# Shifting the tiles behind h by 32 bytes in SBUF, so that they start on multiples of 64 bytes

## The chip, the cores and the metric

The kernel runs on one core of one Trainium2 chip. The metric is the device time of one execution in microseconds (us), as the median of several runs. Shares and clocks come from one profiled execution of the same program.

## What is computed

One layer of a hybrid decoder block, for a sequence of 512 rows of width 1024, all in fp32:

```
mod  = silu(c) @ w_ada + b_ada;  shift, scale, gate = split(mod, 3)
h    = rmsnorm(x, norm_g) * (1 + scale) + shift            # 512 x 1024
proj = h @ w_in                                            # 512 x 14344
qm,km,vm,om,zm,im,fm,qa,ka,va,za,gm,ga = split(proj)
qm, km = split(silu(causal_dwconv([qm, km])))
ym = (head_rmsnorm(sigmoid(om) * mlstm(qm,km,vm,im,fm)) * silu(zm)) @ w_proj_m
ya = (head_rmsnorm(diff_attention(qa,ka,va)) * silu(za)) @ w_proj_a
y  = sigmoid(gm) * ym + sigmoid(ga) * ya
out = rmsnorm(x + gate * (y @ w_out), final_g)
```

The matrix memory (mLSTM) has 4 heads, the differential attention 8. By far the most arithmetic is in `h @ w_in`.

## The kernel before

Each fp32 matrix is split into a high and a low part, and a product is made of three matmuls (`mm3`, lines 133 to 142): high by high, high by low, low by high, all into one PSUM tile. In a matmul one operand is loaded into the array as weights (128 columns of it) and the other moves through it (up to 512 columns).

h is kept as two tiles, `h_hi` and `h_lo`, each 8 blocks of 128 x 512, 16384 bytes per partition. The weight matrix is read in 112 pieces of 128 x 1024 (4096 bytes per partition). Each piece passes through a ring of three buffers each (`raw` for the fp32 data as loaded by SyncE's queue, `whi` and `wlo` for its two parts): ScalarE rounds `raw` to `whi` (line 100), VectorE makes `wlo` as the difference (line 118). Then TensorE uses it in one of two ways: `proj_b` (lines 343 to 352) takes ring columns as weights and moves h over them, 24 matmuls of 512 columns for a piece; `mm_v` (lines 354 to 358) takes h as weights and moves ring columns, 48 matmuls of 256 columns for a piece. `attn_proj` and `proj_m` (lines 706 and 744) take ring columns as weights and move `hh` and `hl`, tiles behind h. The attention and mLSTM cores, cut into small steps by generators that `tick()` calls, fill in between. The order of instructions on each engine is the program's own, with some manual dependencies that keep it.

SBUF is laid out in the order in which pools and tiles are made, each tile at a multiple of 32 bytes of a partition. First come the tiles of the pool `const`: the small ones made before h (`sm`, `ident`, `onesf`, `ones_r`, `mod` and others), then an unused tile of 32 bytes (line 338), then `h_hi` at byte 10784 and `h_lo` at 27168, both 32 past a multiple of 64, then a second unused tile of 32 bytes (line 341) and the few small tiles made later (`acol` and others). Behind `const` lies the pool `stg` with the weight ring, from byte 43808, 32 past a multiple of 64, and behind that the pool `sb` with all others. Within both pools every tile that a matmul reads is as large as a multiple of 64 bytes or follows such tiles, so all of them start 32 bytes past a multiple of 64; and the slices that a matmul takes of them begin at multiples of 64 bytes from the start.

Of the kernel before, what the change touches and what calls it, by code (L numbers as in the profile page):

```python
# [9 lines left out]
F32 = mybir.dt.float32  # L10
# [6 lines left out]
P = 128  # L17
# [48 lines left out]
def hybrid_block_kernel(ctx: ExitStack, tc: tile.TileContext, xT, x, c, wada2, wada, win, wif, wpm, wpa, wout,  # L66
# [3 lines left out]
    const = ctx.enter_context(tc.tile_pool(name="const", bufs=1))  # L70
# [196 lines left out]
    for k in range(NK):  # L267
        i, start = (0, k == 0) if k < 5 else (1, k == 5)
# [69 lines left out]
    const.tile([P, 8], F32, name="pad_before")  # L338
    h_hi = const.tile([P, NK, S], F32R, name="h_hi")
    h_lo = const.tile([P, NK, S], F32R, name="h_lo")  # L340
    const.tile([P, 8], F32, name="pad_after")

    def proj_b(col, between=None):
        hi, lo = split_granule(win[GIDX[("B", col)]])
# [242 lines left out]
    for k in range(NK):  # L587
# [23 lines left out]
        else:  # L611
            csl2.append(sb.tile([P, S], F32, tag="hp", bufs=16, name=nm("csl")))
            i = k - NK + 2
# [454 lines left out]
```

## Time and profile before

| | |
|---|---|
| median of 3 runs | 930.69 us (928.89 to 931.09) |
| the profiled execution | 929.48 us, its span 927.3 us |
| TensorE busy | 914.2 us, 99% of the span, 4735 matmuls |
| VectorE busy | 603.1 us, 65% |
| ScalarE busy | 455.0 us, 49% |
| granted TensorE clock, mean | 0.998 of full |

A busy time counts an engine's own instructions and not its waits. Matmuls are pipelined: one is shown with a duration of some 390 ns while the next starts after some 227 ns, so the distance between starts, not the duration, tells how fast they go. Weight loads have an engine label of their own (PEld) and run beside the matmuls. In the names of a group, the part behind the arrow lists what is read (`acc<-h_hi,whi`), in no order that tells which moves; the width does (512 columns: h moves; 256 columns with h: ring columns move).

### The profile page before, as it was taken

How to read it: one execution, taken by the hardware profiler on the slowest of the kernel's cores; microseconds unless marked ns; L12 is line 12 of the kernel's file. 1: busy time of each engine (PE TensorE's matmuls, PEld its weight loads, DVE VectorE, ACT ScalarE, POOL GpSimd, SP SyncE). 2: the span in 40 equal slices, each digit the busy share in tenths (PEclk: the TensorE clock that was granted, in tenths of full speed). 3: DMA queues.
4: the chain of work that ended last, by engine and by line, in shares of the span. 5: the costliest groups of instructions: out<-in, count | busy, mean ns of one | idle time of the engine just before them, and what ended most of it. 6: DMA issues, size and time to landing. Idle time of an engine off the chain costs nothing.

```text
span 927.3 us, 12276 instructions
## 1 busy us (share of the span) xinstructions
PE 914.2 (99%) x4735; PEld 781.6 (84%) x4735; DVE 603.1 (65%) x975; ACT 455.0 (49%) x741; POOL 24.2 (3%) x56
## 2 busy tenths in 40 slices
PE   7999999999999999999999999999999999999997
PEld 3888987988888899888899888898888988888886
DVE  7967888877675465334568444595554866638944
ACT  7556887766667454222356333453233643137422
POOL 0000010000001000000000000000000000000000
PEclk9999999999999999999999999999999999999999
DMA  9873314434332443332222222222131224426421
GB/s 341 335 199 110 132 58 137 143 119 148 125 102 80 138 147 111 139 136 91 91 83 100 91 81 99 70 102 103 69 114 69 92 97 154 142 108 222 142 77 59
DMA packets 40659, 114.95 MB, mean 124 GB/s; under 512 B 8289, under 2 KB 8553, under 8 KB 39578
## 3 DMA queue, kind: packets, MB, share of 16 engines
q1 hardware_dynamic: 40010, 113.11, 35.1%
q10 hardware_dynamic: 592, 1.07, 0.4%
q8 instruction: 37, 0.61, 0.3%
q14 instruction: 20, 0.16, 0.1%
HBM read 106.78 MB, written 10.00 MB: 126 GB/s over the span
## 4 chain that ended last, share of the span: by engine, by line
PE 94%; DVE 2%; DMA 2%; ACT 1%; issue 0%; SPq 0%; ACTq 0%; DVEq 0%
PE acc L135 26%; PE acc L136 26%; PE acc L137 26%; PE core L135 4%; PE core L136 4%; PE core L137 4%; PE core L444 1%; PE core L445 1%; PE core L474 1%; DMA relt<-in_relb_dram 1%; DVE wlo L118 1%; DMA xt<-in_xT_dram 1%; PE core L238 0%; ACT whi L100 0%; DMA raw<-in_win_dram 0%
## 5 line engine op out<-in xcount | busy, mean ns | idle before, releaser
L135 PE MATMUL acc<-h_hi,whi 128*128 128x512 f32 x688 | 269.2, 391 | 0.5 <-DVE qk L412 0.5
L118 DVE TENSOR_TENSOR wlo<-raw,whi 128x1024 fp32r<-128x1024 f32 x129 | 157.7, 1223 | 164.8 <-ACT whi L100 164.8
L100 ACT CAST whi<-raw 128x1024 fp32r<-128x1024 f32 x129 | 135.4, 1049 | 254.0 <-PE acc L136 204.1
L136 PE MATMUL acc<-h_lo,whi 128*128 128x512 f32 x656 | 256.0, 390 | 0.0
L137 PE MATMUL acc<-h_hi,wlo 128*128 128x512 f32 x656 | 255.5, 389 | 0.0
L135 PEld LDWEIGHTS acc<-h_hi,whi 128*128 128x128 f32 x688 | 129.3, 188 | 26.3 <-PE acc L524 0.8
L137 PEld LDWEIGHTS acc<-h_hi,wlo 128*128 128x128 f32 x656 | 123.2, 188 | 26.0
L136 PEld LDWEIGHTS acc<-h_lo,whi 128*128 128x128 f32 x656 | 123.3, 188 | 23.7
L137 PE MATMUL acc<-whi,h_lo 128*128 128x256 f32 x352 | 99.6, 283 | 0.0
L136 PE MATMUL acc<-wlo,h_hi 128*128 128x256 f32 x352 | 99.6, 283 | 0.0
L135 PE MATMUL acc<-whi,h_hi 128*128 128x256 f32 x352 | 99.5, 283 | 0.0
L135 PE MATMUL acc<-hh,whi 128*128 128x512 f32 x192 | 74.8, 389 | 0.0
L136 PE MATMUL acc<-hl,whi 128*128 128x512 f32 x192 | 74.8, 389 | 0.0
L137 PE MATMUL acc<-hh,wlo 128*128 128x512 f32 x192 | 74.7, 389 | 0.0
L136 PEld LDWEIGHTS acc<-wlo,h_hi 128*128 128x128 f32 x352 | 67.4, 192 | 0.7
L135 PEld LDWEIGHTS acc<-whi,h_hi 128*128 128x128 f32 x352 | 67.4, 191 | 0.7
L137 PEld LDWEIGHTS acc<-whi,h_lo 128*128 128x128 f32 x352 | 67.4, 192 | 0.0
L449 ACT ACTIVATE pt<-pt,mn 128x128 f32<-128x128 f32 (+3 forms) x64 | 35.5, 557 | 17.6 <-DVE mn L447 17.4
L137 PEld LDWEIGHTS acc<-hh,wlo 128*128 128x128 f32 x192 | 36.0, 188 | 7.6
L135 PEld LDWEIGHTS acc<-hh,whi 128*128 128x128 f32 x192 | 36.1, 188 | 7.3
L136 PEld LDWEIGHTS acc<-hl,whi 128*128 128x128 f32 x192 | 36.1, 188 | 7.2
L447 DVE CUSTOM_DVE_ANT_0 pt<-core,bt 128x128 f32<-128x128 f32 (+3 forms) x64 | 29.4, 485 | 15.2 <-PE core L445 14.8
(277 smaller groups left out, 1359.9 us busy)
## 6 DMA issues: line engine op xcount, KB each, us to landing
raw<-in_win_dram SPq DMA_DIRECT2D x112, 512.0 KB, 3.3
wa<-in_wada_dram SPq DMA_DIRECT2D x8, 1024.0 KB, 7.0
raw<-in_wpm_dram SPq DMA_DIRECT2D x16, 512.0 KB, 3.3
raw<-in_wada_dram SPq DMA_DIRECT2D x8, 512.0 KB, 3.2
raw<-in_wpa_dram SPq DMA_DIRECT2D x8, 512.0 KB, 3.2
raw<-in_wout_dram SPq DMA_DIRECT2D x8, 512.0 KB, 3.3
gt_d<-tmp SPq DMA_DIRECT2D x12, 256.0 KB, 2.2
toe_d<-rev_d SPq DMA_DIRECT2D x8, 320.0 KB, 6.4
```

Of the source, the lines that this page charges most:

```text
L100: recent["act"] = nc.scalar.copy(dst, src)
L118: recent["dve"] = nc.vector.tensor_tensor(lo, src, hi.bitcast(F32), ALU.subtract)
L135: a = nc.tensor.matmul(ps, lhs[0], rhs[0], start=start, stop=False)
L136: b = nc.tensor.matmul(ps, lhs[l[0]], rhs[l[1]], start=False, stop=False)
L137: c = nc.tensor.matmul(ps, lhs[r[0]], rhs[r[1]], start=False, stop=stop)
L444: inorder(nc.tensor.matmul(ps, q[m][:, qs], kh[m][:, 0:wn], start=True, stop=False))
L445: inorder(nc.tensor.matmul(ps, q[m][:, qs], kl[m][:, 0:wn], start=False, stop=True))
L447: nc.vector.tensor_tensor_reduce(pp, ps[:, 0:w], bt[:, S - w:S], 1.0, BIG, ALU.add, ALU.min, mn[:, qb, m:m + 1])
L449: nc.scalar.activation(pp, pp, AF.Exp, scale=-1.0, bias=mn[:, qb, m:m + 1], accum_out=ls[:, qb, m:m + 1])
L474: inorder(nc.tensor.transpose(ps[:, n:n + P], pt[:, 0, o:o + P], ident))
```

## The change

A second unused tile of 32 bytes is made behind h. h and all that lies ahead of it stay where they are. The later `const` tiles, the weight ring and all tiles of the pool `sb` lie 32 bytes further on; the ring starts at 43840, a multiple of 64, and so do the other tiles that matmuls read behind h. Instructions, their order, their waits and their operands' shapes are the same.

```
     const.tile([P, 8], F32, name="pad_before")
     h_hi = const.tile([P, NK, S], F32R, name="h_hi")
     h_lo = const.tile([P, NK, S], F32R, name="h_lo")
-    const.tile([P, 8], F32, name="pad_after")
+    for i in range(2):
+        const.tile([P, 8], F32, name=f"pad_after_{i}")
```

## Rows read from the trace of the kernel before

**Rows 1.** The page: span, busy time by engine, granted clock by slice, chain.
```profile
span 927.3 us, 12276 instructions
...
PE 914.2 (99%) x4735; PEld 781.6 (84%) x4735; DVE 603.1 (65%) x975; ACT 455.0 (49%) x741; POOL 24.2 (3%) x56
...
PEclk9999999999999999999999999999999999999999
...
PE 94%; DVE 2%; DMA 2%; ACT 1%; issue 0%; SPq 0%; ACTq 0%; DVEq 0%
```
**Rows 2.** Stretches: length, busy us (instructions) by engine, clock, DMA share, GB/s.
```profile
0.00:25.00 25.00, 19.03 (x48) 9.72 (x49) 18.51 (x33) 19.19 (x29) 0.70 (x6) 1.00 0.92 346
...
400.00:600.00 200.00, 200.00 (x1037) 172.72 (x1036) 108.80 (x141) 78.04 (x114) 4.00 (x8) 1.00 0.27 93
```
**Rows 3.** Matmul groups by shape: count, busy us, mean ns, idle before.
```profile
L135 PE MATMUL acc<-h_hi,whi 128*128 128x512 f32 x688 | 269.2, 391 | 0.5 <-DVE qk L412 0.5
L136 PE MATMUL acc<-h_lo,whi 128*128 128x512 f32 x656 | 256.0, 390 | 0.0
L137 PE MATMUL acc<-h_hi,wlo 128*128 128x512 f32 x656 | 255.5, 389 | 0.0
L137 PE MATMUL acc<-whi,h_lo 128*128 128x256 f32 x352 | 99.6, 283 | 0.0
...
L135 PE MATMUL acc<-hh,whi 128*128 128x512 f32 x192 | 74.8, 389 | 0.0
...
L136 PE MATMUL acc<-h_hi,wlo 128*128 128x512 f32 x32 | 12.5, 389 | 0.0
...
L137 PE MATMUL core<-whi,h_lo 128*128 128x256 f32 x32 | 9.1, 283 | 0.0
```
**Rows 4.** Timeline of TensorE, 512 columns, 24 matmuls apart: start, duration in us.
```profile
300.54 0.39 PE L135 MATMUL acc<-h_hi,whi 128*128 128x512 f32 x1
...
305.98 0.39 PE L135 MATMUL acc<-h_hi,whi 128*128 128x512 f32 x1
```
**Rows 5.** Timeline of TensorE, 256 columns; the last is 48 matmuls on.
```profile
504.21 0.28 PE L135 MATMUL acc<-whi,h_hi 128*128 128x256 f32 x1
504.33 0.28 PE L136 MATMUL acc<-wlo,h_hi 128*128 128x256 f32 x1
...
509.97 0.40 PE L135 MATMUL acc<-hh,whi 128*128 128x512 f32 x1
```
**Rows 6.** Timeline of weight loads beside rows 5.
```profile
504.22 0.19 PEld L136 LDWEIGHTS acc<-wlo,h_hi 128*128 128x128 f32 x1
```
**Rows 7.** Timeline of TensorE after a break at 200.29; rows 9 and 10 matmuls apart.
```profile
200.61 0.40 PE L136 MATMUL acc<-h_lo,whi 128*128 128x512 f32 x1
200.84 0.40 PE L137 MATMUL acc<-h_hi,wlo 128*128 128x512 f32 x1
201.08 0.40 PE L135 MATMUL acc<-h_hi,whi 128*128 128x512 f32 x1
...
202.69 0.39 PE L136 MATMUL acc<-h_lo,whi 128*128 128x512 f32 x1
...
204.96 0.39 PE L137 MATMUL acc<-h_hi,wlo 128*128 128x512 f32 x1
```
**Rows 8.** Timeline of TensorE, first 256-column matmuls after 512-column ones.
```profile
915.29 0.28 PE L135 MATMUL core<-h_hi,yh 128*128 128x256 f32 x1
915.40 0.28 PE L136 MATMUL core<-h_lo,yh 128*128 128x256 f32 x1
915.52 0.28 PE L137 MATMUL core<-h_hi,yl 128*128 128x256 f32 x1
```
**Rows 9.** The page: VectorE's and ScalarE's largest groups, the ring's loads.
```profile
L118 DVE TENSOR_TENSOR wlo<-raw,whi 128x1024 fp32r<-128x1024 f32 x129 | 157.7, 1223 | 164.8 <-ACT whi L100 164.8
L100 ACT CAST whi<-raw 128x1024 fp32r<-128x1024 f32 x129 | 135.4, 1049 | 254.0 <-PE acc L136 204.1
...
raw<-in_win_dram SPq DMA_DIRECT2D x112, 512.0 KB, 3.3
```

## The prediction

> **What bounds the kernel now.** I read four views in this order: the page's totals and chain, the busy time by stretch, the groups of instructions by shape, and the timeline of TensorE (with its weight loads) at three places. The page shows TensorE busy in 914.2 of 927.3 us, 99% of the span, and the chain that ended last lies on it for 94%; VectorE has 2%, DMA 2%, ScalarE 1% [rows 1]. The granted clock is full, the 2.4 GHz level, in all 40 slices. By stretch it is the same: in the 200 us from 400 TensorE is busy all the time, while the DMA share is 0.27; only in the first 25 us is TensorE short (19.03 us busy) and DMA near its limit (share 0.92) [rows 2]. So a change counts as far as it moves the spacing of matmuls, and hardly otherwise.
>
> That spacing is the number to read. Nearly all of the 4735 matmuls come in two widths [rows 3]. In a settled stretch the 512-column ones start at 300.54 and, 24 matmuls on, at 305.98: 5.44 us / 24 = 226.7 ns [rows 4]. The 256-column ones go from 504.21 to 509.97 in 48 matmuls: 5.76 / 48 = 120.0 ns [rows 5]. The difference, 106.7 ns for 256 columns, is 0.417 ns per column, one column per cycle at 2.4 GHz. What is left is the same for both: 226.7 - 512 x 0.417 = 13.3 ns per matmul, whatever its width. Over 4735 matmuls that is 63 us that the columns don't explain.
>
> Where do the 13.3 ns come from? The load of the next weights starts within 0.01 us of each matmul (504.21 and 504.22) and takes 0.19 us [rows 5, 6]; so two streams read SBUF at once, the moving columns and the next 128 columns of weights. And the left-over isn't a constant: right after a break, from 200.61 to 202.69, nine matmuls of the same form on the same tiles stand 2.08 / 9 = 231.1 ns apart, and the next ten (to 204.96) 2.27 / 10 = 227.0 [rows 7]. Nothing differs between the two stretches but how the streams stand to one another in time. At the other end, the first 256-column matmul after wider ones is followed after 0.11 us instead of 0.12 [rows 8]. I read this as two streams that disturb each other, settle after some ten matmuls, and then repeat. A repeating pattern between two address streams can depend on where the streams start.
>
> **The change part by part.** No instruction is added, removed or moved, no wait and no transfer; 32 bytes of SBUF are left empty. Three relations change.
>
> (1) *Between h and the tiles behind it.* Before, both start 32 bytes past a multiple of 64. After, h does still and the tiles behind it start on a multiple of 64, so one stream is displaced by eight fp32 columns against the other. This hits each matmul with one operand in h and the other behind it. From the groups: 688 + 656 + 656 + 2 x 32 = 2064 that move h over ring weights, and 3 x 352 + 3 x 32 = 1152 that move ring columns over h as weights, together 3216 [rows 3]. Some 130 smaller ones of the same kind I leave out. Matmuls with both operands behind h (3 x 192 of the attention output projection [rows 3], the cores, most of the output) keep their relation.
>
> The trace has no pair of streams that stand 32 bytes apart, so the price is bounded from rows. Dearest: the longest step in the unsettled stretch, 0.24 us (200.84 to 201.08 [rows 7]), taken as 236 ns since the rows are rounded: +9.3 ns, 3216 x 9.3 = +30 us. Cheapest: the 0.11 us step [rows 8], taken as 113 ns, against 120: -6.7 ns, 3216 x -6.7 = -21.5 us. Nothing excludes a gain, since the left-over of 13.3 ns is larger than that. In between is nothing at all. I take the mean of the unsettled stretch, 231.1 - 226.7 = +4.4 ns, because it is the only row of any length in which these very matmuls run with the streams displaced against each other, though displaced in time; 3216 x 4.4 = +14.2 us.
>
> The Trainium skill speaks against any price: in "TensorE: Matmul & The Clock Gate", Step-by-step, it says that TensorE has two independent read ports, and that loading the next weights takes no read bandwidth from the running matmul. By that rule the sum is 0. The same page (Wait — 56ns, not 53.3ns?) gives about 2.5 ns as the fixed cost of a matmul; the settled trace has 13.3 ns and the unsettled one 17.7, so here the rule doesn't cover all that is seen, and I don't go by it alone.
>
> (2) *The absolute start of moving columns behind h.* If only the start of the moving stream counted, 1152 + 3 x 192 = 1728 matmuls would be hit [rows 3], at the same bounds: 1728 x 9.3 = +16 us to 1728 x -6.7 = -11.6 us. In the forecast this is not added to (1): they are two readings of one left-over.
>
> (3) *Elementwise work and transfers.* VectorE's and ScalarE's tiles move by 32 bytes too. Their large instructions take 1223 and 1049 ns [rows 9] and lie beside TensorE; of the chain they have 3%, 28 us [rows 1]. If the shift changed each of these by 2% either way, that is 0.6 us; with the cover gone it would be 2% of 603 us. The transfers land 512 KB in 3.3 us [rows 9] as 4096-byte rows per partition. Rows that start on a multiple of 64 touch 64 pieces of 64 bytes instead of 65; if each cost the same, 1.5% of the 21 us in which the first loads are awaited, 0.3 us. I cost both at nothing and keep +-1 us.
>
> Sum: the profiled execution took 929.48 us (span 927.3 and 2.2 around it); + 14.2 = 943.7. That execution is 1.2 us under the median of the three timed runs, 930.69, so the forecast against the median is 945 us, 1.5% slower.
>
> **The rivals.**
> *No change.* The disturbance comes from pieces of 32 bytes or less (or from the start of each load alone), so a displacement by 32 bytes brings the same pattern back; or the left-over is a fixed cost of exchanging weights. For it: 226.7 ns holds alike for h over ring weights and, by the counts and durations, for hh over ring weights (389 to 391 ns [rows 3]), although these tiles lie at different distances. Against it: all of these distances are multiples of 64. Time: 929.7 to 931.7, 931.
>
> *Faster: the streams no longer meet.* With eight columns between them the two streams fall into the pattern of the 0.11 us step and stay there. The place is the same 3216 matmuls, the price -6.7 ns each, and it decides as soon as the settled spacing is below 226 and 119 ns: 929.5 - 21.5 + 1.2 = 909. For it: a 13.3 ns left-over with a row that shows half of it gone. Against it: that step is always a single one at a change of width; the next is 0.12 again [rows 8].
>
> *Faster: moving columns that start on a multiple of 64.* A stream of 2048 or 1024 bytes that starts 32 past a multiple of 64 touches one 64-byte piece more than it needs; a piece at 0.417 ns per column is 6.7 ns. The 1728 matmuls of (2) would lose that: 919. For it: the left-over doesn't depend on the width, as the cost of an end piece wouldn't. Against it: the unsettled rows, which it doesn't explain. The contrary, a price of 4.4 ns for those 1728, would give 938, and is one of the slower cases.
>
> *Much slower: another settled pattern.* The pattern settles one 64-byte piece (6.7 ns) later for all 3216: + 21.5 us, 952. This stands within the slower case, as its upper part.
>
> **How the numbers follow.** Chances: slower through relation (1) or (2), from 936 to 961, 0.46, with 945 as its most direct sum; no change 0.26; streams that no longer meet 0.17; aligned moving columns 0.11. 0.3% is 2.8 us, about what a measurement of this kernel can tell from no change (the three runs span 2.2 us). So faster 0.28, same 0.26, slower 0.46. Cases of both signs hold much of the chance, so the range spans them: from 909, the cheap bound, to 961, the dear bound (929.5 + 30 + 1.2); I leave out 0.05 to 0.1 at each end. The likeliest case by itself reaches from 936 to 961.
>
> **What would show it.** In the changed kernel's timeline, the settled spacing of 512-column matmuls of h over ring weights (24 of one projection) is over 229 ns, that of 256-column ones over 122, while hh over ring weights keeps 226.7 if relation (1) is the cause, and is displaced with the 256-column ones if (2) is. The clock stays at full, the DMA row and the groups of VectorE and ScalarE keep their means within 2%, and TensorE keeps 99%. I am wrong if the spacings are 226.7 and 120.0 again (no change), if they are below, or if the time moves while they stand still; in that case the cause would be in the elementwise work or the transfers, which I costed at nothing.

## The result and the profile after

The changed kernel takes 938.34 us in the median of three runs (938.15 to 938.62) against 930.69: the ratio is 1.0084, 95% interval 1.0069 to 1.0099. It is slower, by 0.8% instead of the 1.5% that were forecast; the profiled execution's span grew by 9.2 us, from 927.3 to 936.5.

The page after the change: span, busy time by engine, the clock by slice, the chain.

```profile
span 936.5 us, 12276 instructions
...
PE 923.8 (99%) x4735; PEld 778.9 (83%) x4735; DVE 603.3 (64%) x975; ACT 455.2 (49%) x741; POOL 24.6 (3%) x56
...
PEclk9999999999999999999999999999999999999999
...
PE 94%; DVE 2%; DMA 2%; ACT 1%; issue 0%; SPq 0%; DVEq 0%
```

Beside [rows 1]: TensorE's busy time is up by 9.6 us with the same 4735 matmuls; VectorE's and ScalarE's are up by 0.2 each, the clock is full as before, the chain has the same shares. So the loss lies with TensorE and, with the same number of matmuls, in the distance between their starts. 8.4 of the 9.2 us lie between the first matmul that reads h (it starts at 21.1 us before and at 21.8 after) and the last matmul; the other 0.7 us is lost ahead of it. That part is scatter: over six of the runs here this first start lies anywhere from 19.7 to 22.4 us. The groups by shape (count, busy us, mean ns):

```profile
L135 PE MATMUL acc<-h_hi,whi 128*128 128x512 f32 x688 | 272.8, 397 | 0.3 <-DVE qk L413 0.3
L136 PE MATMUL acc<-h_lo,whi 128*128 128x512 f32 x656 | 259.4, 395 | 0.0
L137 PE MATMUL acc<-h_hi,wlo 128*128 128x512 f32 x656 | 259.4, 395 | 0.0
L137 PE MATMUL acc<-whi,h_lo 128*128 128x256 f32 x352 | 98.2, 279 | 0.0
L135 PE MATMUL acc<-hh,whi 128*128 128x512 f32 x192 | 74.8, 389 | 0.0
```

Against [rows 3]: h over ring weights is up by 5 to 6 ns, ring columns over h are *down* by 4 (these are durations), and hh over ring weights hasn't changed. The timeline gives the spacing itself: first 24 matmuls of h over ring weights, then 48 of ring columns over h, then 12 of hh over ring weights (start and duration in us, first and last of each).

```profile
304.00 0.40 PE L135 MATMUL acc<-h_hi,whi 128*128 128x512 f32 x1
...
309.60 0.40 PE L135 MATMUL acc<-h_hi,whi 128*128 128x512 f32 x1
```

```profile
509.24 0.28 PE L135 MATMUL acc<-whi,h_hi 128*128 128x256 f32 x1
...
514.84 0.40 PE L135 MATMUL acc<-hh,whi 128*128 128x512 f32 x1
```

```profile
516.21 0.39 PE L135 MATMUL acc<-hh,whi 128*128 128x512 f32 x1
...
518.93 0.39 PE L135 MATMUL acc<-hh,whi 128*128 128x512 f32 x1
```

5.60 / 24 = 233.3 ns instead of 226.7 [rows 4]; 5.60 / 48 = 116.7 instead of 120.0 [rows 5]; 2.72 / 12 = 226.7 as before. The two classes in which one operand lies in h and the other behind it have moved, one up, one down; the class with both behind it has not.

### The profile page after: what moved, and what is told of

Its sections match the earlier page's. It is cut to its first block, busy times and chain, and to the rows that moved or that the text cites. A ratio compares the mean times of both kernels' runs of the same rounds, so it can differ in the third digit from the quotient of the medians.

```text
span 936.5 us, 12276 instructions
## 1 busy us (share of the span) xinstructions
PE 923.8 (99%) x4735; PEld 778.9 (83%) x4735; DVE 603.3 (64%) x975; ACT 455.2 (49%) x741; POOL 24.6 (3%) x56
## 4 chain that ended last, share of the span: by engine, by line
PE 94%; DVE 2%; DMA 2%; ACT 1%; issue 0%; SPq 0%; DVEq 0%
PE acc L135 26%; PE acc L136 26%; PE acc L137 26%; PE core L135 4%; PE core L137 4%; PE core L136 4%; PE core L445 1%; PE core L446 1%; PE core L475 1%; DMA relt<-in_relb_dram 1%; DMA xt<-in_xT_dram 1%; DVE wlo L118 1%; PE core L238 0%; DMA raw<-in_win_dram 0%; PE core L331 0%
## 5 line engine op out<-in xcount | busy, mean ns | idle before, releaser
L135 PE MATMUL acc<-h_hi,whi 128*128 128x512 f32 x688 | 272.8, 397 | 0.3 <-DVE qk L413 0.3
L118 DVE TENSOR_TENSOR wlo<-raw,whi 128x1024 fp32r<-128x1024 f32 x129 | 157.7, 1223 | 170.8 <-ACT whi L100 170.7
L100 ACT CAST whi<-raw 128x1024 fp32r<-128x1024 f32 x129 | 135.1, 1047 | 262.7 <-PE acc L136 209.4
L136 PE MATMUL acc<-h_lo,whi 128*128 128x512 f32 x656 | 259.4, 395 | 0.0
L137 PE MATMUL acc<-h_hi,wlo 128*128 128x512 f32 x656 | 259.4, 395 | 0.0
L136 PEld LDWEIGHTS acc<-h_lo,whi 128*128 128x128 f32 x656 | 123.4, 188 | 27.0
```

The lines of the kernel that those rows point to most:

```text
L100: recent["act"] = nc.scalar.copy(dst, src)
L118: recent["dve"] = nc.vector.tensor_tensor(lo, src, hi.bitcast(F32), ALU.subtract)
L135: a = nc.tensor.matmul(ps, lhs[0], rhs[0], start=start, stop=False)
L136: b = nc.tensor.matmul(ps, lhs[l[0]], rhs[l[1]], start=False, stop=False)
L137: c = nc.tensor.matmul(ps, lhs[r[0]], rhs[r[1]], start=False, stop=stop)
```

## The experiments

The theory: what counts is the distance in SBUF between the two streams that TensorE reads at once, the moving columns and the next weights. Distances are given modulo some number of bytes, that is, as the remainder after division by it. The rivals: the absolute place of h or of the ring; the other tiles that moved, with ScalarE's and VectorE's writes and the transfers; and, for the theory's own form, after how many bytes the pattern repeats.

**Both unused tiles left out: h at a multiple of 64, the rest 32 past one.**

```
-    const.tile([P, 8], F32, name="pad_before")
     h_hi = const.tile([P, NK, S], F32R, name="h_hi")
     h_lo = const.tile([P, NK, S], F32R, name="h_lo")
-    const.tile([P, 8], F32, name="pad_after")
```

> Both unused tiles are left out: h starts on a multiple of 64 bytes, the ring and all behind it 32 bytes past one; the two have changed places against the changed kernel, and the distance modulo 64 is again 32. Theory (only the distance of the two streams modulo 64 counts): 512-column matmuls of h over ring weights at 233 ns, 256-column ones at 117, hh over ring weights at 227, time 0.8% over before, about 938 us. Rival (it is the absolute place, h 32 past a multiple of 64 with the ring on one): spacings of 226.7 and 120.0 and the time of before, 931 us.

Measured: 940.7 us, ratio 1.0112 (1.0091 to 1.0132), above the expected 938. The groups of h over ring weights have the means of the changed kernel, though h and ring have changed places modulo 64; ring columns over h came down less than there.

```profile
L135 PE MATMUL acc<-h_hi,whi 128*128 128x512 f32 x688 | 272.6, 396 | 0.3 <-DVE qk L410 0.3
...
L137 PE MATMUL acc<-whi,h_lo 128*128 128x256 f32 x352 | 98.9, 281 | 0.0
...
L135 PE MATMUL acc<-hh,whi 128*128 128x512 f32 x192 | 74.8, 390 | 0.0
```

The absolute place falls as the cause. That the 256-column ones differ from the changed kernel's (281 against 279 ns long, and settled at 118.3 against 116.7 ns between starts) says that a distance of 32 and one of -32 aren't the same, which a period of 64 bytes would make them.

**Only the unused tile ahead of h left out: all at multiples of 64.**

```
-    const.tile([P, 8], F32, name="pad_before")
     h_hi = const.tile([P, NK, S], F32R, name="h_hi")
```

> Only the unused tile ahead of h is left out: h, the ring and all behind it start on multiples of 64 bytes. Theory (distance modulo 64): the distance is 0 as before, so 226.7 and 120.0 ns and 931 us, within 0.3%. Rival (absolute place: a ring on multiples of 64 is dear): 233 and 117 ns, 938 us.

Measured: 929.31 us, ratio 0.9992 (0.9982 to 1.0002): the same. The groups are those of [rows 3]:

```profile
L135 PE MATMUL acc<-h_hi,whi 128*128 128x512 f32 x688 | 269.1, 391 | 0.5 <-DVE qk L411 0.5
...
L137 PE MATMUL acc<-whi,h_lo 128*128 128x256 f32 x352 | 99.6, 283 | 0.0
```

So a start at a multiple of 64 is neither good nor bad; the ring lies on one here, as in the changed kernel, and costs nothing.

**Three unused tiles behind h: the rest 64 bytes further on than before.**

```
-    const.tile([P, 8], F32, name="pad_after")
+    for i in range(3):
+        const.tile([P, 8], F32, name=f"pad_after_{i}")
```

> Three unused tiles behind h instead of one: all behind h lies 64 bytes further on than before, h stays. Theory (the pattern repeats every 64 bytes): 226.7 and 120.0 ns, 931 us, within 0.3% of before. Rival (a period of 128 bytes or more, or any shift of the ring costs): the spacing of h over ring weights moves by more than 2 ns and the time by over 0.5%.

Measured: 940.27 us, ratio 1.0110 (1.0090 to 1.0129). The expectation missed: 64 bytes cost at least as much as 32. 24 matmuls of h over ring weights:

```profile
303.60 0.39 PE L135 MATMUL acc<-h_hi,whi 128*128 128x512 f32 x1
...
309.20 0.39 PE L135 MATMUL acc<-h_hi,whi 128*128 128x512 f32 x1
```

5.60 / 24 = 233.3 ns. A period of 64 bytes falls; "multiples of 64" in the change's name isn't what matters.

**Sixteen places in steps of 4 bytes, ring buffers 64 bytes larger.**

```
+    def ring(tag, name=None, off=0):
+        return stg.tile([P, D + 16], F32R, tag=tag, name=name or nm(tag))[:, off:off + D]
...
+        off = seen[kind] % 16
+        seen[kind] += 1
+        hi, lo = ring("whi", off=off), ring("wlo", off=off)
```

> Ring tiles 64 bytes larger; each piece's high and low part begin 0, 4, 8, ... 60 bytes into their tile, in turn, so the distance to h (and to hh) takes all sixteen values of fp32 columns. Theory (distance modulo 64, from reads of 64-byte pieces): spacing of h over ring weights is 227 at 0 and about 233 at 32, of 256-column ones 120 and 117, and in between it changes by steps at multiples of 16 or 32 bytes. Rival (the pattern has the period of 32 bytes with two states at random): offsets of 0 and 32 don't differ systematically. Time between 927 and 945 us, not used.

One time, 944.67 us; not conclusive. With buffers of 4160 bytes the three buffers of the ring, and `whi` and `wlo`, lie at different distances modulo 128, so that a place within a buffer isn't one distance; even in five pieces at 0 the settled matmuls of h over ring weights stood 226.6 ns apart in one and 233 to 234 in the others. The next runs keep all places with buffers of 4608 bytes.

**Only the pieces used as weights under h, 32 bytes into their buffers** (buffers of 4608 bytes here and below, `D + 128`; a piece for `proj_b` is of kind B, one for `proj_v` of kind A, the others keep 0).

```
+        off = 8 if kind == "B" else 0
```

> The layout is that of before, with ring buffers 512 bytes larger (4608, so that all places modulo 512 are kept); only the pieces that are used as weights under h (82 pieces, 1968 matmuls of 512 columns) are written and read 32 bytes into their buffers. Theory (the spacing is set by the distance of the two streams that TensorE reads at once; it is 226.7 only where the distance is a multiple of 128 or 256 bytes): those matmuls at 233 ns, +5.5 to 6 each, +11 to 12 us, 941 to 943 us; the 256-column ones stay at 120, hh over ring weights at 227. Rival (the other tiles that moved, or the writes of ScalarE and VectorE and the transfers, made the difference): time of before, 930 us.

Measured: 940.64 us, ratio 1.0114 (1.0098 to 1.0130), just under the expected 941 to 943. Modulo 512, nothing has moved but these pieces within their buffers.

```profile
L135 PE MATMUL acc<-h_hi,whi 128*128 128x512 f32 x688 | 272.9, 397 | 0.4 <-DVE qk L415 0.4
L136 PE MATMUL acc<-h_lo,whi 128*128 128x512 f32 x656 | 259.6, 396 | 0.0
...
L137 PE MATMUL acc<-whi,h_lo 128*128 128x256 f32 x352 | 99.6, 283 | 0.0
```

The loss is that of the weights' distance to h, and larger than the change's, because the 256-column ones don't gain here.

**Only the pieces whose columns move over h, 32 bytes into their buffers.**

```
+        off = 8 if kind == "A" else 0
```

> As the run with shifted weights, but only the pieces whose columns move over h as weights (22 pieces, 1056 matmuls of 256 columns) lie 32 bytes into their buffers. Theory: these go from 120 to about 117 ns as in the changed kernel, -3 each, -3.1 us, 927 us (0.3% faster); 512-column ones stay at 226.7. Rival (a shift of the ring costs whatever its use): slower than before, or the same.

Measured: 927.05 us, ratio 0.9965 (0.9951 to 0.9979): faster than both kernels. 36 matmuls of ring columns over h:

```profile
504.76 0.28 PE L135 MATMUL acc<-whi,h_hi 128*128 128x256 f32 x1
...
508.96 0.39 PE L135 MATMUL acc<-hh,whi 128*128 128x512 f32 x1
```

4.20 / 36 = 116.7 ns, and h over ring weights is as before (391, 390 and 390 ns). The change holds both: h over ring weights, which loses, and ring columns over h, which gain.

**The changed kernel with the weights put back.**

```
     h_lo = const.tile([P, NK, S], F32R, name="h_lo")
-    const.tile([P, 8], F32, name="pad_after")
+    for i in range(2):
+        const.tile([P, 8], F32, name=f"pad_after_{i}")
...
+        off = 56 if kind == "B" else 0
```

> The changed kernel, with ring buffers 512 bytes larger, in which the 82 pieces used as weights under h lie 224 bytes into their buffers, so that their distance to h is a multiple of 256 bytes again; all other tiles stay where the change put them. Theory: h over ring weights returns from 233 to 226.7 ns for 1968 matmuls, -11 us; the 256-column ones keep their 117: 927 us, faster than before by about 0.3%. Rival (the other tiles that the change moved carry a part of the loss): 930 to 938 us.

Measured: 928.41 us, ratio 0.9982 (0.9972 to 0.9991): the loss is gone, and a gain of 0.2% is left instead of 0.3; the two intervals overlap. By the starts in the trace, ring columns over h keep their whole gain (116.8 ns in the mean against 119.8 before); what is missing is spread over the other matmuls in amounts under 1 us. 24 matmuls of h over ring weights:

```profile
304.23 0.39 PE L135 MATMUL acc<-h_hi,whi 128*128 128x512 f32 x1
...
309.67 0.39 PE L135 MATMUL acc<-h_hi,whi 128*128 128x512 f32 x1
```

5.44 / 24 = 226.7 ns. Here the ring pieces used as weights lie 0 bytes from h modulo 512; in the kernel before they lie 256 from it, and the spacing is the same.

**Eight places in steps of 32 bytes.**

```
+        off = 8 * (seen[kind] % 8)
+        seen[kind] += 1
```

> Buffers of 4608 bytes; each piece lies 0, 32, 64, ... 224 bytes into its buffer, in turn, by kind. Theory with a period of 128 bytes: h over ring weights settles at 226.7 at 0 and at 128, and stays at 231 to 236 at the six others. Rival, a period of 256 bytes or more: settled at one of 0 and 128 alone, at 233 at the other. Rival, history (what ran before a piece decides, not the place): no order by place.

Each piece's settled spacing is worked out from its start times in the trace: matmuls 13 to 24 of a piece of h over ring weights, 25 to 48 of one of ring columns over h; a figure is the mean of the pieces at its place. In ns:

```
place in the buffer (bytes)     0     32     64     96    128    160    192    224
h over ring weights         226.7  233.3  233.3  234.2  233.1  233.3  229.3  233.3
ring columns over h         120.0  116.6  117.8  119.9  118.7  117.8  113.3  118.3
```

Two pieces of h over ring weights in the timeline, 12 matmuls apart each; the first lies at 0, the second at 128.

```profile
618.73 0.39 PE L135 MATMUL acc<-h_hi,whi 128*128 128x512 f32 x1
...
621.45 0.39 PE L135 MATMUL acc<-h_hi,whi 128*128 128x512 f32 x1
...
833.43 0.39 PE L135 MATMUL acc<-h_hi,whi 128*128 128x512 f32 x1
...
836.23 0.39 PE L135 MATMUL acc<-h_hi,whi 128*128 128x512 f32 x1
```

2.72 / 12 = 226.7 and 2.80 / 12 = 233.3: a period of 128 bytes falls as well. 256 fits all the runs up to here: h over ring weights settles at 226.7 ns at a distance of 256 modulo 512 (the kernel before) and at 226.5 to 226.8 in all 78 pieces at 0 (the changed kernel with the weights put back). There is order by place: nearly all pieces at one place have the same spacing, so history isn't the main cause. It isn't without effect either: at 192, nine of the ten pieces of h over ring weights settle at 229 ns and one at 233.

**All places in steps of 4 bytes, below 128 and from 128 on.**

```
+        off = seen[kind] % 32
```
```
+        off = 32 + (seen[kind] * (13 if kind == "A" else 1) + (16 if kind == "A" else 0)) % 32
```

> Buffers of 4608 bytes; each piece lies 0, 4, 8, ... 124 bytes into its buffer, in turn, by kind. Theory (only a distance of a multiple of 128 settles): 226.7 at 0, over 229 at the 31 others for h over ring weights; 256-column ones between 113 and 122 by place. Rival (other distances settle too, some lower): a place where the last 12 of 24 spacings are alike and under 226.7.

> Buffers of 4608 bytes; each piece lies 128, 132, ... 252 bytes into its buffer, in turn, by kind (the moving ones in steps of 52 bytes, from 192). Theory (512-column matmuls settle low only at a multiple of 256 bytes; 256-column ones have several settled spacings): h over ring weights at 229 to 235 at nearly all, no place under 226.7; 256-column ones 113 to 125, at 192 again 113.3. Rival (there are places under 226.7 between 128 and 252): one where the last 12 of 24 spacings lie alike under 226.7.

Single times of 941.98 and 941.61 us. For h over ring weights the settled spacing was 226.7 at 0, but also at 120, 132, 156, 204 and 240, and in one piece of two or three at 12, 40 and 244, where the others stood at 230 to 234; elsewhere 229 to 237; nowhere less. So "only multiples of 256" falls, though no place beats 0. For ring columns over h it lay between 113.3 (at 192 again) and 123.4 (at 4), in no order that we could read.

**Moving columns at 192, and a way into its better pattern.**

```
+        off = 48 if kind == "A" else 0
```

> As the run with shifted moving columns, but those 22 pieces lie 192 bytes into their buffers, the place at which the scan in steps of 32 bytes showed 113.3 ns. Theory: the 1056 matmuls of 256 columns settle at 113.3 instead of 120.0, -6.7 each, -7.0 us: 923.4 us, 0.75% faster than before; all 512-column groups stay at 226.7 to 227.7. Rival (the 113 ns came from the neighbours in the scan and don't hold, or a later wait takes the gain): 927 to 930 us.

Measured: 927.18 us, ratio 0.9969 (0.9957 to 0.9981): no better than 32 bytes, so the expected 923.4 missed. The timeline shows why; here are the last 12 steps of two pieces at the same place, up to the matmul that follows the piece.

```profile
94.20 0.28 PE L135 MATMUL acc<-whi,h_hi 128*128 128x256 f32 x1
...
95.56 0.39 PE L447 MATMUL core<-qk,qk 128*128 128x512 f32 x1
...
100.72 0.28 PE L135 MATMUL acc<-whi,h_hi 128*128 128x256 f32 x1
...
102.14 0.38 PE L477 MATMUL core<-ident,pt 128*128 128x128 f32 x2
```

1.36 / 12 = 113.3 in the first, 1.42 / 12 = 118.3 in the second (117.8 from the unrounded starts). At this place two patterns last; 4 of the 22 pieces fell into the cheap one, and none of the 15 that come right behind h over ring weights at 226.7. The last run tried to lead into it:

```
+                split(hi[:, 8:264], lo[:, 8:264], raw[:, 0:256], eng="act")
+                split(hi[:, 304:1072], lo[:, 304:1072], raw[:, 256:D], eng="act")
...
+            at = 8 if kk == 0 else 48 + kk * 256
+            wsl = slice(at, at + 256)
```

> As the run with moving columns at 192 bytes, but the first quarter of such a piece (12 matmuls) lies 32 bytes into its buffer and the other three quarters 192; the split of these 22 pieces is made in two parts on ScalarE and VectorE, 44 instructions more. Theory (at 192 two patterns exist, 113.3 and 117.8 ns, and which one a piece settles in depends on what ran before it; after a settled 512-column stream it is 117.8): the unsettled first quarter leads into 113.3 for the other 36 matmuls, -4.4 each in 18 pieces, -3 us against that run: 924 us. Rival (117.8 is reached from there too): 927 us; or the added instructions make a piece late: slower than 927.

Measured: 926.92 us, ratio 0.9969 (0.9959 to 0.9979). The rival held: 6 of 22 pieces settled at 113.3, the rest at 117.8. All 15 pieces right behind h over ring weights went to 117.8 again; of the seven behind other matmuls, six now went to 113.3. The first quarter runs at about 117 ns in all 22, so its spacing alone doesn't tell which pattern follows; what is handed over from one stretch to the next was not found.

## Why the prediction came out as it did

*The bound* was read rightly: the loss is in TensorE's spacing. VectorE's and ScalarE's busy times have moved by 0.2 us, GpSimd's by 0.4, and the clock not at all.

*Relation (1)* is the cause, shown from three sides: shifted weights alone lose 10 us, shifted moving columns alone gain 3, and the changed kernel with its weights put back is no longer slower. Relation (2), the absolute start, was excluded by hh over ring weights and by the kernel with everything on multiples of 64. Part (3), costed at nothing, was nothing that can be seen: VectorE's and ScalarE's large instructions take 1223 and 1047 ns after 1223 and 1049, and a load of 512 KB still lands in 3.3 us.

*The price* was the mis-sized term. The prediction took +4.4 ns for all 3216 matmuls, the mean of an unsettled stretch. In fact the displaced streams settle too, at +6.7 ns for h over ring weights, which was the price of the "much slower" case, and at -3.3 for ring columns over h. Over all matmuls of the two classes, those near a break included, the mean steps are 227.7 to 233.2 and 119.8 to 116.9 (each from the start times of both traces): 2064 x 5.5 = +11.4 and 1152 x -2.9 = -3.3, together +8.1. Of the rest of the 9.2 us some 0.7 is the later start of the first matmul with h, and the smaller matmuls that were left out bring some tenths.

The forecast of +14.2 had the first class too cheap, 2064 x 4.4 = +9.1, and the second with the wrong sign, 1152 x 4.4 = +5.1: an unsettled stretch of 512-column matmuls says nothing of the price in 256-column ones. By the prediction's own sign, a spacing over 122 for that class, it was wrong there. The two errors pull against each other, so that the total came as near as it did is partly luck; the way it went was right because the class that loses is both larger and dearer. The settled prices, +6.7 and -3.3, lie within the bounds of -6.7 to +9.3. The row behind the dear bound was misread by rounding: from the unrounded starts the step from 200.84 to 201.08 is 233 ns and not 236, but the step after it has 236, so the bound stands. Between medians the change is 7.7 us, the difference to the spans being their scatter.

*Against "no change"* the prediction argued that the distances of h and hh to the ring are multiples of 64 and therefore say nothing of 32. That was right in effect and too narrow: they are multiples of 256, and for h over ring weights 64 and 128 cost as much as 32.

*The faster rival*, streams that fall into the 0.11 us step and stay, isn't fanciful: it happens at 192 bytes, for the 256-column ones, in some pieces.

The Trainium skill ("SBUF — State Buffer", Who interferes with whom) says that TensorE never waits on anyone. Whether another engine's access to SBUF can hold it up is not what these runs test. They show that its own matmuls change their pace with the distance of their two operands: with nothing moved modulo 512 but the weights' place, 226.7 became 233.3 ns. Whoever reads that sentence as one on time would have called the change free.

What stays open: how the distance acts. The runs show that it sets the spacing, and at which distances, but no rule that gives the cheap ones. That the two streams collide while they are read at the same time is an inference: every matmul here has a weight load of its own beside it (4735 of each), and a kernel in which the same columns move with no load beside them was not tried.

## What to carry to other kernels

In a kernel that is bound by matmuls with a weight load beside each, read the settled spacing from start times, take off the time of the columns, and ask what the rest depends on; the distance in SBUF between moving and weight tiles is one such thing, worth 3% of a 512-column step here and 3 to 6% of a 256-column one. Set it for each use by itself, with an offset within a buffer, rather than by moving whole pools: the simplest of the fastest versions here (927.05 us) keeps h over ring weights at 0 modulo 256 and puts only the moving columns 32 bytes on; the two with 192 bytes (927.18 and 926.92) can't be told from it. Check that the buffers of a ring are all at the same distance; with buffers of 4160 bytes, no multiple of 256, they were not.

## What the runs showed of the hardware

The settled spacing of back-to-back matmuls with a weight load beside each depends on the distance in SBUF between the moving columns and the weights: 226.7 to 237 ns for 512 columns and 113.3 to 123.4 for 256, at the same full clock. The common values, 113.3, 116.7, 120.0 and 226.7, 233.3, differ by some 3.3 or 6.7 ns, but others, such as 117.8 and 230.0, lie between them.

A settled stretch is one that repeats, not one of equal steps. In the run with places in steps of 32 bytes, the unrounded starts of h over ring weights show steps of 226 and 227 ns at 0. At 32 bytes steps of 235 and 232 ns alternate. At 128 some pieces alternate between 229 and 238, and others repeat every seven steps. At 192 steps of 226, 229 and 232 repeat every three. So two or three steps don't tell the pace; here 12 or 24 are taken.

At one place two settled patterns can exist: 113.3 and 117.8 ns at 192 for ring columns over h, 229 and 233 at 192 for h over ring weights. Which one comes goes with what ran before: behind h over ring weights at 226.7 it was 117.8 in 15 pieces of 15.
